# Branch A's scores: products over 64 rows, one component on each half of TensorE's rows, in place of products over 128 rows

## The chip, the cores and the metric

The kernel runs on one core of one Trainium2 chip. The metric is the device time of one execution in microseconds (us): the median of the timed runs. All times in the text are from these runs, or from one execution that the hardware profiler recorded.

## The reference, cut to what is computed

One layer of a streaming encoder with two attention branches beside each other, for a prompt of 2048 frames and for 8 running streams of 16 new frames with 512 cached frames each. The change concerns branch A alone, and of it the prompt's frames:

```python
D_MODEL, SEQ, CHUNK, Q_BLOCK = 1024, 2048, 64, 128
N_HEADS_A, HEAD_DIM_A = 4, 64

def diff_attention(q, k, v, qpos, kpos, lam):          # q, k: (b, s, heads, 2 components, 64)
    s = einsum('bqhcd,bkhcd->bhcqk', q, k) * (HEAD_DIM_A ** -0.5)
    mask = (kpos // CHUNK)[None, :] <= (qpos // CHUNK)[:, None]
    p = softmax(where(mask, s, -inf), axis=-1)
    w = p[:, :, 0] - lam * p[:, :, 1]
    return einsum('bhqk,bkhe->bqhe', w, v)             # v: (b, s, heads, 128)
```

Each of the four heads has two components c (0 and 1) with 64 numbers each for a query and for a key. The scores are a product over these 64 numbers for each component. Branch B (stick-breaking attention, eight heads of 64) has scores of the same shape with other weights behind them. Before the attention stand a norm and a projection (2048 x 1024 by 1024 x 6144), behind it gates, two branch products and one output product.

## The kernel before, in words

**Number format.** A float32 operand is cut into two fp16 halves, `hi` and `lo` (`split`: ScalarE writes hi = scale * x, VectorE writes lo = scale * x - hi). A product of two such numbers is made of three: hi*hi, hi*lo and lo*hi.

**Units and tiles.** The attention is done in eight units u of two heads of B or one head of A: even units are branch A (`kind` 0), odd ones branch B (`kind` 1). A unit has 17 steps, one for each tile t of 128 rows: the sample tile (t = NT = 16) first, and then the 16 prompt tiles. Per step there are
- `project`: 24 matmuls of 512 columns into a bank "mm" of PSUM, most steps 24 more for the gates into bank "t"; then in `finish` the rotation of q and k on GpSimd (A only), and the cutting into halves: `query` for q, `halves` for k and v;
- `transpose_qk`: TensorE turns the halves of q and k into bank "t", 128 x 128 a block, and ScalarE (A) or VectorE (B) copies them into `kst` (k) and `qst` (q), which have the 64 numbers along the rows;
- `scores`: for prompt tile t there are t // 4 + 1 chunks of 512 keys (the last one of 128 to 512). Its inner `chunk(c, ch)` makes one component's (in B: one head's) scores of one chunk in one bank "s". In the last chunk, the mask is added by one more product;
- `evacuate` (A): VectorE reads the bank, scales it into the score buffer and keeps the largest value; behind the last chunk `softmax_pair` queues exp, sums, the difference of the two components, its halves and their turn by a DMA, and 27 cost units later the products with v (`pv_block`), three a block of 128 keys.

**A's operands before.** k is turned as two blocks, one for each component, with rows [hi 64; lo 64]. q is turned as four blocks: for each component [hi; hi] and [lo; 0]. So the first product of `chunk` (L708) gives hi*hi + hi*lo over 128 rows and the second (L709) lo*hi, with 64 rows times zero:

```python
            T.matmul(p[:, 0:n], qst[:, c, :], kk[:, c, 0:n], start=True, stop=False)
            T.matmul(p[:, 0:n], qst[:, 2 + c, :], kk[:, c, 0:n], start=False, stop=not diag)
```

**What sets the order.** Pieces of the projection, the scores and the products with v are interleaved by costs that the code gives them (`interleaved`, `give`, `later_on`). The framework then puts each engine's instructions in order by its own model of the time; an engine runs them in that order. `kept` holds an instruction in the order of the code. PSUM has 8 banks: 2 "mm", 3 "s", 1 "t", 2 "o". A buffer taken anew waits until its last reader is done, so the fourth score bank taken waits for the evacuation of the first.

## Time and profile before

| | |
|---|---|
| timed runs | 2225.53 us median of 3 (2224.59 to 2226.76) |
| the profiled execution: its time, first to last instruction | span 2223.5 us (no other time of it is recorded) |
| TensorE matmuls, busy | 2061.2 us (93%), 14608 matmuls |
| TensorE weight loads, busy (beside the matmuls) | 1110.4 us (50%) |
| VectorE, busy | 1743.8 us (78%) |
| ScalarE, busy | 1606.2 us (72%) |
| GpSimd, busy | 699.6 us (31%) |
| mean granted TensorE clock | 0.980 |

The span lies about 2 us below the median of the timed runs. A matmul's record has a length in which its way through the array is included (383 ns for 512 columns), and the records of a stream overlap: the next starts 216 ns after the one before. So what a matmul costs in a stream is read from starts in the timeline, not from its length. PE is TensorE's matmuls, PEld its weight loads, DVE VectorE, ACT ScalarE, POOL GpSimd.

### The profile page before, as it was taken

The page shows a single profiled execution, that of the slowest core. Times are in us where ns is not written, and L with a number is a line of the kernel's source. Part 1 is how long each engine was busy: PE and PEld are TensorE (multiplying, and loading weights), DVE is VectorE, ACT ScalarE, POOL GpSimd, SP SyncE. Part 2 cuts the span into 40 slices and gives each one's busy share as a digit, 9 for nine tenths or more (in the row PEclk, how much of TensorE's full clock was granted, in tenths as well). Part 3 has the DMA queues.
Part 4 walks back from the last instruction along what each step waited for, and adds up shares of the span by engine and source line. Part 5 has one row for each costly group of instructions (what it writes and reads, how often), then busy time and mean ns, then how long its engine had stood idle before and what let it go on. Part 6 is the DMA issues. An engine that isn't in the chain of part 4 may idle for free. (4 is left out here: it accounts for less than half of the span.)

```text
span 2223.5 us, 41495 instructions
## 1 busy us (share of the span) xinstructions
PE 2061.2 (93%) x14608; PEld 1110.4 (50%) x14608; DVE 1743.8 (78%) x3799; ACT 1606.2 (72%) x3212; POOL 699.6 (31%) x608
## 2 busy tenths in 40 slices
PE   5999999999999999999999998989998788899997
PEld 3655555555555455555554554555454444444443
DVE  4667869789887788988778888777789877787864
ACT  3978677789877677978677788876688666666531
POOL 1232014356410443742024355301334412111210
PEclk8999999999999999999999999999999899999999
DMA  9778559899796889979879999985787999999762
GB/s 323 258 241 201 120 139 217 181 227 203 200 252 158 222 201 202 207 205 221 198 195 216 191 224 207 241 181 130 159 170 155 201 280 255 230 254 224 194 166 67
DMA packets 824978, 451.05 MB, mean 203 GB/s; under 512 B 556122, under 2 KB 763274, under 8 KB 824256
## 3 DMA queue, kind: packets, MB, share of 16 engines
q1 hardware_dynamic: 823820, 448.01, 82.7%
q8 instruction: 114, 1.87, 0.3%
q14 instruction: 96, 0.79, 0.1%
q10 hardware_dynamic: 948, 0.39, 0.1%
HBM read 229.87 MB, written 86.02 MB: 142 GB/s over the span
## 5 line engine op out<-in xcount | busy, mean ns | idle before, releaser
L688 POOL TENSOR_TENSOR sc_p<-sc_p,sc_n 128x127 f32<-128x127 f32 (+7 forms) x192 | 313.3, 1635 | 663.1 <-DVE sc_n L682 510.6
L467 PEld LDWEIGHTS <-hs 128*128 128x128 f16 x3120 | 293.3, 99 | 318.5 <-issue 6.4
L467 PE MATMUL ps_mm<-wa,hs 128*128 128x512 f16 x1590 | 391.2, 382 | 5.3 <-DMA hs<-hT_d 5.0
L467 PE MATMUL ps_mm<-wb,hs 128*128 128x512 f16 x1530 | 377.4, 380 | 0.0
L682 DVE TENSOR_TENSOR_SCAN sc_n<-ps_s,sc_n,zero_t 128x512 f32<-128x512 f32 x192 | 245.4, 1278 | 33.3 <-ACT ps_s L134 28.1
L708 PE MATMUL ps_s<-k,qst 128*128 128x512 f16 (+3 forms) x640 | 223.2, 350 | 30.0 <-DVE sc_n L682 22.8
L543 PEld LDWEIGHTS <-hs 128*128 128x128 f16 x1632 | 155.0, 98 | 181.7 <-DVE qst L576 5.1
L543 PE MATMUL ps_t<-wa,hs 128*128 128x512 f16 x1020 | 242.3, 380 | 2.1 <-DVE qst L576 2.0
L619 DVE TENSOR_TENSOR sc_n<-sc_p,sc_n 128x128 f16<-128x128 f32 (+7 forms) x192 | 217.7, 1137 | 32.9 <-ACT sc_n L616 32.3
L134 ACT ACTIVATE sc_p<-ps_s,usc 128x512 f32<-128x512 f32 (+3 forms) x320 | 203.9, 637 | 34.4 <-PE ps_s L709 23.0
L709 PE MATMUL ps_s<-k,qst 128*128 128x512 f16 (+3 forms) x640 | 223.6, 350 | 0.0
L616 ACT CAST sc_n<-sc_p 128x128 f16<-128x128 f32 (+7 forms) x192 | 155.0, 809 | 57.3 <-POOL sc_p L688 55.8
L134 ACT ACTIVATE ps_s<-ps_s,usc 128x512 f32<-128x512 f32 (+3 forms) x320 | 196.3, 613 | 0.0
L543 PE MATMUL ps_t<-wb,hs 128*128 128x512 f16 x612 | 151.7, 383 | 4.8 <-DMA hs<-hT_d 2.1
L769 PE MATMUL ps_o<-v,wt 128*128 128x128 f16 x1088 | 135.2, 224 | 22.1 <-DMA wt<-sc_n 21.9
L1535 PE MATMUL ps_o<-wo,wb 128*128 128x512 f16 x624 | 141.6, 382 | 1.1 <-ACT wb L1309 1.1
L602 DVE TENSOR_SCALAR_CACHE_REDUCE sc_p<-ps_s,usc 128x512 f32<-128x512 f32 (+3 forms) x160 | 106.2, 664 | 35.7 <-PE ps_s L709 20.5
L770 PE MATMUL ps_o<-v,wt 128*128 128x64 f16 x1088 | 127.1, 196 | 0.0
L769 PEld LDWEIGHTS <-wt 128*128 128x128 f16 x1088 | 101.0, 100 | 50.1 <-DMA wt<-sc_n 25.3
L682 DVE TENSOR_TENSOR_SCAN sc_n<-ps_s,zero_t 128x128 f32<-128x128 f32 (+3 forms) x128 | 104.0, 813 | 27.7 <-ACT ps_s L134 27.7
L1501 PEld LDWEIGHTS <-wa 128*128 128x128 f16 x816 | 77.7, 98 | 94.2 <-issue 4.1
L1544 POOL TENSOR_TENSOR x<-m,x 128x512 f32<-128x512 f32 x32 | 45.6, 1427 | 247.1 <-DVE m L1539 138.7
(378 smaller groups left out, 4548.6 us busy)
## 6 DMA issues: line engine op xcount, KB each, us to landing
hs<-hT_d SPq DMA_DIRECT2D x132, 512.0 KB
g_d<-gt SPq DMA_DIRECT2D x68, 256.0 KB
out_dram<-pr SPq DMA_DIRECT2D x204, 64.0 KB
o_d<-o SPq DMA_DIRECT2D x136, 64.0 KB
wa<-g_d SPq DMA_DIRECT2D x17, 512.0 KB
wb<-g_d SPq DMA_DIRECT2D x17, 512.0 KB
hs<-o_d SPq DMA_DIRECT2D x17, 512.0 KB
wide<-in_w_ada_dram SPq DMA_DIRECT2D x8, 1024.0 KB
```

The source lines that it names most:

```text
L134: i = S.activation(**kw)
L467: T.matmul(box["p"], box["h"][:, hi, k, :], U["w"][k][:, wi, :], start=(n == 0), stop=(n == 3 * KT - 1))
L543: x = T.matmul(box["g"][:, 0:gw], box["h"][:, hi, k, :], U["wg"][k // per][:, k % per, wi, :], start=(j == 0), stop=(j == 3 * KT - 1))
L616: x = S.copy(out=hi, in_=src)
L619: V.tensor_tensor(out=lo, in0=src, in1=hi, op=ALU.subtract)
L682: V.tensor_tensor_scan(out=dst[:, lo : lo + n][:, ::-1], data0=src[:, 0:n][:, ::-1], data1=zero_t[:, 0:1].to_broadcast([P, n]), initial=fi ...
L688: G.tensor_tensor(out=p[:, 0:m], in0=p[:, 0:m], in1=n[:, 1 : m + 1], op=ALU.mult)
L708: T.matmul(p[:, 0:n], qst[:, c, :], kk[:, c, 0:n], start=True, stop=False)
L709: T.matmul(p[:, 0:n], qst[:, 2 + c, :], kk[:, c, 0:n], start=False, stop=not diag)
L769: T.matmul(po[:, c * P : (c + 1) * P], wt[:, wj, :], vt[:, c, :, :], start=first, stop=False)
L770: T.matmul(po[:, c * P : c * P + 64], wt[:, nb + wj, :], vt[:, c, 0, :], start=False, stop=last)
L1535: T.matmul(po, st["y"][:, yi * 8 + k, :], wo[j * 4 + k // 2][:, wi, k % 2, :], start=(n == 0), stop=(n == 3 * KT - 1))
```

## The change

For the prompt tiles of branch A only:
- q and k are cut into halves so that one block has the hi halves of both components and one the lo halves (`by_half`: columns c = 0, then c = 1, taken in the same buffers). `query`'s doubled hi (128 x 256 on ScalarE) becomes a plain cut of 128 x 128.
- `transpose_qk` turns four blocks (k hi, k lo, q hi, q lo), not six, and the copy of q has 256 columns, not 512. Behind the turn, rows 0 to 63 are component 0 and rows 64 to 127 component 1.
- `pair(ch)` replaces `chunk(0, ch)` and `chunk(1, ch)`: it takes two banks "s" at once, then issues a product of one column into the first bank (128 rows; its result is overwritten), six products of 64 rows (three a component, the components in turn, in the order of the code by `kept`), the masks in the last chunk, and both evacuations.

B's scores and the sample tile's are as before.

```diff
+    def by_half(qb, k16):
+        return qb[:, 0, :, :, :].rearrange("p c r d -> p c (r d)"), k16.rearrange("p c f d -> p c (f d)")
...
-                query(rot[:, 0:128], s)
-                halves(k16, rot[:, 128:256], s)
+                if t == NT:
+                    query(rot[:, 0:128], s)
+                    halves(k16, rot[:, 128:256], s)
+                else:
+                    qn, kn = by_half(qb, k16)
+                    split(qn[:, 0, :], qn[:, 1, :], rot[:, 0:128], s, S)
+                    split(kn[:, 0, :], kn[:, 1, :], rot[:, 128:256], s, S)
...
+        paired = U["kind"] == 0 and t < NT
+        if paired:
+            qn, kn = by_half(q16, k16)
+            for j, x in enumerate((kn[:, 0, :], kn[:, 1, :], qn[:, 0, :], qn[:, 1, :])):
+                T.transpose(pt[:, j * P : (j + 1) * P], x, id16)
...
-        copy(out=qst, in_=pt[:, 256:768].rearrange("p (j n) -> p j n", j=4))
+        nq = 2 if paired else 4
+        copy(out=qst, in_=pt[:, 256 : 256 + nq * P].rearrange("p (j n) -> p j n", j=nq))
...
+        def pair(ch):
+            job = own[0]
+            seg = job["segs"][ch * 4 // SEG]
+            n = 512 if ch < t // 4 else (t % 4 + 1) * P
+            ps = [bank("s"), bank("s")]
+            qst, kk = U["q", t], U["k"][ch]
+            diag = ch == t // 4
+            T.matmul(ps[0][:, 0:1], idb, mask_a[:, 0:1], start=True, stop=True)
+            for i, (qf, kf) in enumerate(((0, 0), (0, 1), (1, 0))):
+                for c in (1, 0):
+                    rows = slice(c * 64, c * 64 + 64)
+                    x = T.matmul(ps[c][:, 0:n], qst[rows, qf, :], kk[rows, kf, 0:n], start=(i == 0), stop=(i == 2 and not diag))
+                    kept(x)
+            if diag:
+                for c in range(2):
+                    T.matmul(ps[c][:, n - 64 : n], idb, mask_a, start=False, stop=True)
+            for c in range(2):
+                evacuate(job, seg, c, ps[c], ch * 512 - seg["lo"] * P, n, sc[:, 3:4], sc[:, 4:5], ch)
+            if diag:
+                softmax_pair(job)
...
+        if kind == 0:
+            return [(4.0 if ch < t // 4 else t % 4 + 1.0, lambda ch=ch: pair(ch)) for ch in range(nch)]
```

In the built program the order of all engines is laid out anew. Three places show it. (In the rows, the line of the code comes first, then the operation, out<-in and the size; the number behind a name counts buffers as they are taken, so two numbers of ps_s are two banks taken.)

TensorE, unit 0, tile 5, the first chunk of 512 keys, component 0. Before, its two products (L708, L709) stand between products with v (L765 to L767), and those of component 1 come 48 rows later:

```order
L767 LDWEIGHTS wt_1585
L767 MATMUL ps_o_1982<-v_912,wt_1585 128x128
L708 LDWEIGHTS qst_1686
L708 MATMUL ps_s_1734<-k_977,qst_1686 128x512
L709 LDWEIGHTS qst_1686
L709 MATMUL ps_s_1734<-k_977,qst_1686 128x512
L765 LDWEIGHTS wt_1591
L765 MATMUL ps_o_1991<-v_912,wt_1591 128x128
```

The same chunk now, from the second round of its six products (L764) on; ahead of these rows stand a projection's matmul and the first round:

```order
L764 LDWEIGHTS qst_1693
L764 MATMUL ps_s_1768<-k_975,qst_1693 128x512
L764 LDWEIGHTS qst_1693
L764 MATMUL ps_s_1767<-k_975,qst_1693 128x512
L764 LDWEIGHTS qst_1693
L764 MATMUL ps_s_1768<-k_975,qst_1693 128x512
L764 LDWEIGHTS qst_1693
L764 MATMUL ps_s_1767<-k_975,qst_1693 128x512
L760 LDWEIGHTS idb_194
L760 MATMUL ps_s_1800<-masks_196,idb_194 128x1
L471 LDWEIGHTS hs2_182
L471 MATMUL ps_mm_2522<-wa3_172,hs2_182 128x512
```

The six stand together (in 157 of the 160 pairs; in three, one matmul of one column of L235 stands between the second and the third round). The product of one column (L760) behind them is that of the next pair: it writes bank 1800, which is taken after 1767 and 1768.

TensorE, unit 0, tile 9, the last chunk (256 keys), and tile 10 behind it. Before, other work stands between component 0 and component 1 of tile 9, and again between tile 9 and tile 10 (7 products with v behind the rows shown):

```order
L712 MATMUL ps_s_2275<-masks_196,idb_194 128x64
L765 LDWEIGHTS wt_2100
L765 MATMUL ps_o_2500<-v_912,wt_2100 128x128
L766 LDWEIGHTS wt_2100
L766 MATMUL ps_o_2500<-v_912,wt_2100 128x128
L767 LDWEIGHTS wt_2100
L767 MATMUL ps_o_2500<-v_912,wt_2100 128x128
L708 LDWEIGHTS qst_2140
L708 MATMUL ps_s_2308<-k_2021,qst_2140 128x256
L709 LDWEIGHTS qst_2140
L709 MATMUL ps_s_2308<-k_2021,qst_2140 128x256
```

Now:

```order
L764 MATMUL ps_s_2330<-k_2041,qst_2162 128x256
L768 LDWEIGHTS idb_194
L768 MATMUL ps_s_2330<-masks_196,idb_194 128x64
L768 LDWEIGHTS idb_194
L768 MATMUL ps_s_2331<-masks_196,idb_194 128x64
L760 LDWEIGHTS idb_194
L760 MATMUL ps_s_2379<-masks_196,idb_194 128x1
L764 LDWEIGHTS qst_2299
L764 MATMUL ps_s_2380<-k_975,qst_2299 128x512
L764 LDWEIGHTS qst_2299
L764 MATMUL ps_s_2379<-k_975,qst_2299 128x512
```

Tile 10's pair follows directly, and its bank 2380 is the one that 2330 was in (three banks in turn). Of the 156 distances from a pair's end to the next pair of the same unit, 8 have less than 1 us of TensorE's work in them (5 of them in unit 0); before, 26 of 156 distances from one chunk's component 0 to the next chunk's had less than 1.2 us.

VectorE, unit 0, tiles 1 and 2. Before, the evacuations (L602) of the two components of tile 1 (256 keys) have nine other rows between them:

```order
L602 TENSOR_SCALAR sc_p_1457,mx_1459<-ps_s_1453,usc0_702 128x256
L636 TENSOR_REDUCE nm_1447<-mx_1440 128x2
L323 SCALAR_TENSOR_TENSOR wb0_1426<-wa7_176,sw_1515,wb0_1426 128x512 x2
L323 SCALAR_TENSOR_TENSOR wb1_1427<-wa6_175,sw_1515,wb1_1427 128x512 x2
L323 SCALAR_TENSOR_TENSOR wb2_1428<-wa5_174,sw_1515,wb2_1428 128x512 x2
L323 SCALAR_TENSOR_TENSOR wb3_1429<-wa4_173,sw_1515,wb3_1429 128x512
L502 SCALAR_TENSOR_TENSOR qbuf1_214<-rot_1846,sq0_711,qbuf1_214 128x2x64
L323 SCALAR_TENSOR_TENSOR wb3_1429<-wa4_173,sw_1515,wb3_1429 128x512
L323 SCALAR_TENSOR_TENSOR k16_1844<-rot_1846,sq0_711,k16_1844 128x2x64
L650 RECIPROCAL r_1450<-l_1449 128x2
L602 TENSOR_SCALAR sc_n_1458,mx_1459<-ps_s_1472,usc0_702 128x256
```

Now (L620 is the same instruction) they follow each other:

```order
L323 SCALAR_TENSOR_TENSOR sc_n_1438<-sc_p_1437,r_1445,sc_n_1438 128x128
L620 TENSOR_SCALAR sc_p_1461,mx_1463<-ps_s_1450,usc0_702 128x256
L620 TENSOR_SCALAR sc_n_1462,mx_1463<-ps_s_1451,usc0_702 128x256
L243 TENSOR_SCALAR sc_q_1498<-ps_t_1496 128x1
L371 COPY fsq_1507<-ps_t_1496 128x1
```

The cutting of the next unit's weights (L323 on wb) has gone to another place.

More of the change, by code (lines that the diff above doesn't have):

```diff
@@ L572, in transpose_qk @@
             U["q", t] = qst = stg.tile([P, 4, P], F16, tag="qst", name="qst", bufs=Q_BUFS)
+            if paired:
+                qst = qst[:, 0:2, :]
             kst = U["k"][g][:, :, i * P : (i + 1) * P]
```

16 lines of the change are left out of this document (8 added, 8 removed).

## The prediction

> **What bounds the kernel now.** I read the page first (busy time by engine), then the busy time in the four stretches in which branch A's scores run, TensorE's waits, the groups by line and shape, and the timeline for what a matmul costs in a stream.
>
> ```profile
> span 2223.5 us, 41495 instructions
> PE 2061.2 (93%) x14608; PEld 1110.4 (50%) x14608; DVE 1743.8 (78%) x3799; ACT 1606.2 (72%) x3212; POOL 699.6 (31%) x608
> core 0: us, PE busy (x) PEld busy (x) DVE busy (x) ACT busy (x) POOL busy (x), PEclk, DMA share, GB/s
> sum 685.00, PE 648.40 PEld 360.22 DVE 558.26 ACT 516.63 POOL 169.37; mean PE 162.10 PEld 90.06 DVE 139.57 ACT 129.16 POOL 42.34
> ```
>
> The last row sums the stretches 130 to 295, 530 to 700, 940 to 1112 and 1354 to 1532 us, the units of branch A. TensorE is busy 648.4 of 685.0 us there, VectorE 81%, ScalarE 75%. So in the stretches that the change touches TensorE is the bound, all other engines together make it idle for 36.6 us, and a microsecond of TensorE's stream is worth nearly a microsecond of time. What it waits for:
>
> ```profile
> PE ps_o L769 <- DMA wt<-sc_n: 21.9, 11, 4.2
> PE ps_o L765 <- DMA wt<-sc_n: 18.3, 14, 5.6
> PE ps_s L708 <- DVE sc_n L602: 4.9, 4, 1.5
> PE ps_s L708 <- DVE sc_p L602: 0.5, 1, 0.5
> ```
>
> (us in total, times, longest.) L765 is branch A's product with v, late for the turn by DMA; L602 is the evacuation of A's scores, for which the next score bank waits: 5.4 us in all, five times.
>
> **The change part by part.** Branch A has four units of 16 tiles with t // 4 + 1 chunks, 40 chunks a unit, 160 in all: 112 of 512 keys and 16 each of 384, 256 and 128. The groups by shape agree (A and B have half each):
>
> ```profile
> L708 PE MATMUL ps_s<-k,qst 128*128 128x512 f16 x448 | 171.5, 383 | 22.8 <-DVE sc_n L682 15.7 <-DVE sc_n L602 4.9 <-DVE csc L951 1.4
> L708 PE MATMUL ps_s<-k,qst 128*128 128x384 f16 x64 | 20.9, 326 | 4.4 <-DVE sc_n L682 4.4
> ...
> 1004.21 0.38 PE L708 MATMUL ps_s<-k,qst 128*128 128x512 f16 x1
> 1004.43 0.38 PE L709 MATMUL ps_s<-k,qst 128*128 128x512 f16 x1
> 1004.65 0.19 PE L712 MATMUL ps_s<-masks,idb 128*128 128x64 bf16 x1
> 1004.67 1.24 PE L467 MATMUL ps_mm<-wb,hs 128*128 128x512 f16 x5
> ...
> 1006.62 0.28 PE L561 MATMUL ps_t<-id,k 128*128 128x128 f16 x2
> 1006.73 0.39 PE L565 MATMUL ps_t<-id,qbuf 128*128 128x128 f16 x4
> 1006.95 0.22 PE L765 MATMUL ps_o<-v,wt 128*128 128x128 f16 x1
> ```
>
> From the starts in the timeline: 512 columns cost (1004.65 - 1004.21) / 2 = 0.22 us, and by the five in a row behind them (1.24 - 0.38) / 4 = 0.215; I use 0.216; the six turns 0.33 / 6 = 0.056 each; the mask of 64 columns 0.03. By proportion 384 columns cost 0.162, 256 cost 0.108, 128 cost 0.056.
>
> *Products.* Before, a chunk is four products: 0.864 us at 512 keys, 0.648, 0.432, 0.224 at the smaller ones. Now it is six of 64 rows. No product on half of the rows next to one on the other half stands in this trace. The nearest rows are products on quarters of TensorE's columns (L860, L883), which are issued in the same way, four in turn, and those with few rows (L1489):
>
> ```profile
> L860 PE MATMUL ps_s<-dks,qpad 128*32 128x512 f16 x256 | 16.8, 381 | 2.9 <-ACT wa L1309 2.9
> ...
> 1807.76 1.24 PE L1535 MATMUL ps_o<-wo,wb 128*128 128x512 f16 x5
> 1808.93 1.05 PE L860 MATMUL ps_s<-dks,qpad 128*32 128x512 f16 x16
> ...
> 1828.31 1.06 PE L1308 MATMUL ps_s<-id,hs 128*128 128x128 f16 x16
> 1829.30 0.84 PE L883 MATMUL ps_t<-v16c,dwt 128*32 128x256 f16 x24
> 1830.07 1.25 PE L1535 MATMUL ps_o<-wo,wb 128*128 128x512 f16 x5
> ...
> 1770.84 1.24 PE L1501 MATMUL ps_mm<-wb,wa 128*128 128x512 f16 x5
> 1772.01 1.12 PE L1489 MATMUL ps_t<-gsm,ones 1*128 1x512 f32 x2
> ```
>
> Sixteen products of 512 columns on quarters take 1.05 us with the last one's length of 0.38: four rounds, (1.05 - 0.38) / 3 = 0.22 a round. So four parts of the array run at once, and a round costs what one matmul does, 0.218. I take the same for two halves of the rows: three rounds a pair, 0.654 at 512 keys. The other end is that they don't overlap: six times 0.216.
>
> *Switches.* The same rows show what it costs to change how the array is divided. Five products of L1535 from 1807.76 are done by 1807.76 + 5 x 0.216 = 1808.84, and L860 starts at 1808.93: 0.09 us. Sixteen turns from 1828.31 end at 1829.21, L883 starts at 1829.30: 0.09; six rounds of 0.109 end at 1829.96, the next full matmul starts at 1830.07: 0.10. For rows instead of columns, L1501's five end at 1771.92 and L1489, on one row, starts at 1772.01: 0.09 again. So a pair pays 0.19 us, in and out. Nothing hides it: TensorE streams on both sides.
>
> [...]
>
> *One-column product (L760).* One a pair; nearest row the mask of 64 columns, 0.03 us. Its wait for a bank stands ahead of everything behind it on TensorE: see the banks below.
>
> *Sum of a pair:* 0.654 + 0.19 + 0.03 = 0.874 against 0.864 at 512 keys, + 0.01, times 112 is + 1.1 us. At 384: 0.164 x 3 + 0.22 = 0.712, + 0.064; at 256: 0.55, + 0.118; at 128: 0.39, + 0.166; together 0.348 x 16 = + 5.6. Three pairs are split by a matmul of full rows (L235) and switch twice more: + 0.6. In all + 7.3 us. The gain of a quarter of the products (29 us) is eaten by 160 x 0.22 = 35 us of switches and one-column products.
>
> *Turns.* Two fewer a tile: 64 x 2 x 0.056 = 7.2 us less on TensorE, all of it in its stream. Products and turns together: + 0.1 us.
>
> *ScalarE.*
>
> ```profile
> L576 ACT COPY qst<-ps_t 128x512 f16<-128x512 f16 x64 | 38.8, 606 | 0.0
> L575 ACT COPY k<-ps_t 128x256 f16<-128x256 f16 x64 | 24.0, 375 | 2.1 <-PE ps_t L565 2.1
> L501 ACT ACTIVATE qbuf<-rot,sq 128x256 f16<-128x256 f32 x68 | 34.7, 510 | 3.2 <-POOL rot L513 2.7
> L318 ACT ACTIVATE k<-rot,sq 128x128 f16<-128x128 f32 x68 | 27.3, 402 | 10.4 <-PE ps_t L561 10.4
> ```
>
> The copy of q goes from 606 ns to that of k's width, 375; the hi half from 510 to 402: 64 x 0.339 = 22 us less on an engine busy 75% there. No wait of TensorE for ScalarE stands among the rows above, so I count 1 us. VectorE's lo halves have as many elements as before; DMAs, SP and POOL have the same work.
>
> *Banks.* Of three score banks a pair takes two at once, so its second waits for the first evacuation of the pair before; a chunk before waited for the one three back.
>
> ```profile
> L602 DVE TENSOR_SCALAR_CACHE_REDUCE sc_p<-ps_s,usc 128x512 f32<-128x512 f32 x112 | 83.4, 745 | 30.0 <-PE ps_s L709 20.5 <-PE ps_s L712 9.0
> L602 DVE DVE_READ_ACCUMULATOR sc_p<-ps_s,usc 128x1 f32 x160 | 12.9, 81 | 0.0
> ```
>
> An evacuation takes 0.745 + 0.081 = 0.83 us and starts when the last product is through (0.16 us behind its stream, 0.38 - 0.22). So behind a pair the next must stand 1 us off or TensorE stops, with all that is queued behind it (projection, turns, products with v). In the order of the changed kernel 8 of 156 distances are shorter: at the 1.2 us that a wait took before (4.9 / 4) that is 9 us if none is softened, and half of it, 5 us, is near the 5.4 us that go away. I take + 1 us, between - 5 (all bank waits gone, since pairs stand further apart elsewhere) and the rival below.
>
> *Sum:* 2223.5 + 0.1 - 1 + 1 = 2223.6, and with 2 us between span and median as before, 2226 us by the timed runs: no change. (About 0.2%, 4.5 us, is what a measurement of this kernel can tell from none.)
>
> **Rivals.**
> 1. *Waits go (faster).* ScalarE is relieved by 22 us of 517 and pairs stand further apart (8 close ones, 26 before). If a third of the 36.6 us of idle TensorE goes, 12 us are saved: 2214 us. For it: the rows of L708 and ScalarE's load. Against it: half of the idle time (18.3 us) is L765's, which waits for the turn by a DMA, and the change leaves that.
> 2. *The second bank (slower).* VectorE is busy 81%; where a long instruction stands ahead of the first evacuation, the pair waits that much longer. If 16 of the 156 pairs wait the 1.2 us of a wait before, that is 19 us against 5.4: + 14, 2240 us. It decides from 9 waits on ((4.5 + 5.4) / 1.2 = 8.3). For it: 8 pairs are too close already. Against it: the other distances are mostly over 2 us, two evacuations.
> 3. *Weights aren't hidden between products of one half (slower).* A round of L860 would show it and doesn't (0.22 with four loads), but these load 32 columns each, a pair's 128. Exposed twice a pair at the 0.1 us of a switch, that is 160 x 0.2 = 32 us: 2258 us. [...]
> 4. *The change doesn't do what it says: halves of rows don't run at once.* Six times 0.216 + 0.22 is 1.516 for 0.864 at 512 keys: 112 x 0.652 = 73 us; at 384, 256 and 128 it is 0.544, 0.436 and 0.332 more, times 16, 21 us. With the split pairs' 0.6 and less the turns' 7.2 that is + 87: 2313 us. For it: no row here has two halves of rows at work. Against it: four quarters of columns do run at once.
> [...]
>
> **How the numbers follow.** Forecast (TensorE's sum is nil, waits within 4 us) 0.36; rival 1, 0.29; rival 5, 0.04; rival 2, 0.22; rival 3, 0.06; rival 4, 0.03. Faster by over 0.2% is 0.29 + 0.04 = 0.33, within it 0.36, slower 0.22 + 0.06 + 0.03 = 0.31. The likeliest is 2226; its own range is 2221 to 2230. The range of 8 in 10 takes in rivals 1 and 2 with their spread of some 8 us about 2214 and 2240: 2206 to 2248; outside are rivals 3 to 5 (0.13) and the tails of 1 and 2.
>
> **What would show it.** Right: products of L764 in three rounds of 0.22 us, two starts a few ns apart; 0.09 us ahead of a pair and 0.10 behind it; a full pair 0.87 us from the matmul ahead to the one behind; turns four a tile; TensorE's busy time in A's stretches unchanged to a few us; its waits for L620 (the evacuation) below 10 us. Wrong: rounds of 0.3 us or more (rivals 3, 4); a gap ahead of pairs other than 0.09; waits of L760 and L764 for VectorE of 15 us and more (rival 2); idle time in A's stretches that falls by 10 us (rival 1). The forecast also falls if the new order of all engines moves the waits in branch B's units, which no row of the profile before can tell.

## The result, and the profile after

The changed kernel takes 2306.89 us (median of 4 runs, 2303.14 to 2309.48), the kernel before 2225.06 us beside it: a ratio of 1.0372, with a 95% interval of 1.0357 to 1.0388. It is slower, by 82 us; the forecast was 2226, the range ended at 2248. One execution of 4331 us, of the run E18 below, is left out of its median. The profiled execution, from its page (span, busy time by engine, and the chain that ended last):

```profile
span 2301.3 us, 42229 instructions
PE 2101.7 (91%) x14960; PEld 1082.7 (47%) x14960; DVE 1764.6 (77%) x3799; ACT 1585.5 (69%) x3212; POOL 715.3 (31%) x608
PE 41%; DVE 19%; DMA 15%; ACT 13%; issue 7%; POOL 3%; SPq 1%; DVEq 0%; POOLq 0%; ACTq 0%
```

TensorE's share of the span fell, and the busy times of the other engines are within 21 us of those before. TensorE's own busy time rose by 40 us (2061.2 before) and its idle time by 37 (162 before, 200 now), though its sum in the prediction is nil. The time at half clock rose from 90 to 153 us (see the table below); that would make some 31 of the 40 us (an estimate: half of the 63 us more, since products of 128 columns started 0.107 us apart at half clock and 0.057 at the full one, by the timeline at the end). The chain passes through four engines and the DMAs, none with half of it. Lines have moved: A's evacuation L602 is now L620, B's scores L708 are L726, B's scan L682 is L700, the products with v L765 and L769 are L806 and L810, the projection L467 is L471, the gates L543 are L552.

**A pair by itself is what was forecast.** TensorE's timeline around one pair of 512 keys (start, length to the end of the last, group):

```profile
1067.11 2.97 PE L471 MATMUL ps_mm<-wb,hs 128*128 128x512 f16 x13
1070.01 0.82 PE L764 MATMUL ps_s<-k,qst 64*128 64x512 f16 x6
1070.77 0.18 PE L760 MATMUL ps_s<-masks,idb 128*128 128x1 bf16 x1
1070.80 0.27 PE L573 MATMUL ps_t<-id,k 128*128 128x128 f16 x2
1070.91 0.27 PE L573 MATMUL ps_t<-id,qbuf 128*128 128x128 f16 x2
```

Thirteen projection products end at 1067.11 + 13 x 0.216 = 1069.92, the pair starts 0.09 us later. From its start to the next full matmul are 0.76 us: six products in three rounds (0.65) and 0.10 to switch back. So 0.85 us with both switches, 0.88 with the one-column product (forecast 0.874). Four blocks are turned where there were six. ScalarE's two steps shrank as forecast (groups by shape; 606 and 510 ns before):

```profile
L594 ACT COPY qst<-ps_t 128x256 f16<-128x256 f16 x64 | 25.2, 393 | 0.0
L318 ACT ACTIVATE qbuf<-rot,sq 128x128 f16<-128x128 f32 x64 | 26.1, 409 | 4.7 <-POOL rot L517 4.7
```

**The waits grew, but not at the pair.** TensorE's longest (total, times, longest):

```profile
PE ps_s L726 <- DVE sc_n L700: 48.3, 44, 3.0
PE ps_o L810 <- DMA wt<-sc_n: 26.8, 18, 4.2
PE ps_o L806 <- DMA wt<-sc_n: 22.9, 18, 2.7
...
PE ps_s L764 <- DVE sc_n L620: 5.5, 8, 1.3
```

L764, the pair, waits 5.5 us for its banks in this row, and 7.6 with two shorter rows (1.4 us of L764 and 0.7 of L760); that was forecast at below 10. Branch B's scores wait 48 us for the scan that reads their banks; the row was 22.8 us before:

```profile
PE ps_s L708 <- DVE sc_n L682: 22.8, 25, 2.2
```

**Where the time is.** I cut both executions at the first score tile of each unit: four stretches of A, three of B (B's fourth runs into the end). Busy time of all engines, the sums; A's four and then B's three, before:

```profile
sum 700.00, PE 663.40 PEld 365.54 DVE 557.46 ACT 533.85 POOL 168.70; mean PE 165.85 PEld 91.38 DVE 139.36 ACT 133.46 POOL 42.17
...
sum 702.00, PE 668.25 PEld 361.88 DVE 591.44 ACT 567.78 POOL 328.35; mean PE 222.75 PEld 120.63 DVE 197.15 ACT 189.26 POOL 109.45
```

and after:

```profile
sum 781.00, PE 742.34 PEld 367.05 DVE 558.37 ACT 517.27 POOL 155.82; mean PE 185.59 PEld 91.76 DVE 139.59 ACT 129.32 POOL 38.95
...
sum 711.00, PE 634.77 PEld 338.10 DVE 614.37 ACT 567.06 POOL 350.96; mean PE 211.59 PEld 112.70 DVE 204.79 ACT 189.02 POOL 116.99
```

A's stretches are 81 us longer, B's three 9 us; the rest is 12 shorter, which makes the 78 us between the spans. And A's stretches hold work that was in B's. The projection's products alone in A's four stretches (length, matmuls' busy time and count, loads', clock), before (1495 products):

```profile
136.00:301.00 165.00, 80.76 (x348) 33.02 (x349) 0.99 0.69 174
531.00:705.00 174.00, 90.70 (x384) 36.17 (x385) 1.00 0.85 208
940.00:1118.00 178.00, 91.42 (x382) 36.25 (x382) 0.99 0.85 206
1355.00:1538.00 183.00, 89.30 (x381) 36.03 (x382) 0.98 0.83 195
```

and after (1708):

```profile
135.00:324.00 189.00, 93.72 (x392) 37.31 (x390) 0.97 0.62 159
558.00:755.00 197.00, 101.28 (x438) 41.04 (x438) 0.99 0.75 193
991.00:1191.00 200.00, 102.44 (x438) 41.24 (x438) 0.99 0.77 190
1432.00:1627.00 195.00, 103.17 (x440) 41.15 (x440) 0.99 0.76 186
```

That is 213 products or 46 us (x 0.216) more. The gates' products were 120 in each stretch before; now they are 144 in three of them and 120 in the fourth, 72 or 16 us more:

```profile
558.00:755.00 197.00, 32.56 (x144) 13.57 (x144) 0.99 0.75 193
...
1432.00:1627.00 195.00, 27.97 (x120) 10.99 (x120) 0.99 0.76 186
```

In the order this shows as a delay: A's last tile was scored at projection step 22.0, 56.0, 90.0 and 124.1 of the kernel's 136, and now at 25.0, 58.8, 92.8 and 126.9 (24 products a step). B's stretches have 33 us less of TensorE's busy time and are no shorter. The mean granted clock fell from 0.980 to 0.967.

### The profile page after: what moved, and what is told of

Read it like the earlier page. It is cut to its first block, busy times and chain, and to the rows that moved or that the text cites. A ratio compares the mean times of both kernels' runs of the same rounds, so it can differ in the third digit from the quotient of the medians.

```text
span 2301.3 us, 42229 instructions
## 1 busy us (share of the span) xinstructions
PE 2101.7 (91%) x14960; PEld 1082.7 (47%) x14960; DVE 1764.6 (77%) x3799; ACT 1585.5 (69%) x3212; POOL 715.3 (31%) x608
## 4 chain that ended last, share of the span: by engine, by line
PE 41%; DVE 19%; DMA 15%; ACT 13%; issue 7%; POOL 3%; SPq 1%; DVEq 0%; POOLq 0%; ACTq 0%
PE ps_mm L471 13%; PE ps_t L552 8%; DMA wt<-sc_n 6%; PE ps_o L1576 5%; DVE sc_n L700 4%; PE ps_mm L1542 4%; ACT sc_p L134 3%; PE ps_s L764 2%; ACT junk L298 2%; POOL sc_p L706 2%; ACT sc_n L134 1%; DVE sc_n L323 1%; DVE sc_p L675 1%; DVE sc_n L637 1%; DVE sc_n L620 1%
## 5 line engine op out<-in xcount | busy, mean ns | idle before, releaser
L706 POOL TENSOR_TENSOR sc_p<-sc_p,sc_n 128x127 f32<-128x127 f32 (+7 forms) x192 | 323.5, 1687 | 480.6 <-DVE sc_n L700 471.7
L471 PEld LDWEIGHTS <-hs 128*128 128x128 f16 x3120 | 294.7, 99 | 333.3 <-issue 29.2
L471 PE MATMUL ps_mm<-wa,hs 128*128 128x512 f16 x1590 | 393.8, 386 | 3.4 <-DMA hs<-hT_d 3.0
L471 PE MATMUL ps_mm<-wb,hs 128*128 128x512 f16 x1530 | 377.3, 385 | 3.6 <-DMA hs<-hT_d 2.2
L700 DVE TENSOR_TENSOR_SCAN sc_n<-ps_s,sc_n,zero_t 128x512 f32<-128x512 f32 x192 | 245.4, 1278 | 38.5 <-ACT ps_s L134 32.2
L637 DVE TENSOR_TENSOR sc_n<-sc_p,sc_n 128x128 f16<-128x128 f32 (+7 forms) x192 | 239.7, 1252 | 23.9 <-ACT sc_n L634 23.7
L552 PEld LDWEIGHTS <-hs 128*128 128x128 f16 x1632 | 156.4, 100 | 194.0 <-issue 14.1
L552 PE MATMUL ps_t<-wa,hs 128*128 128x512 f16 x1020 | 242.8, 385 | 3.3 <-DVE qst L594 2.1
L726 PE MATMUL ps_s<-k,qst 128*128 128x512 f16 (+3 forms) x320 | 112.4, 352 | 59.1 <-DVE sc_n L700 48.3
L810 PE MATMUL ps_o<-v,wt 128*128 128x128 f16 x1088 | 137.3, 225 | 26.9 <-DMA wt<-sc_n 26.8
L552 PE MATMUL ps_t<-wb,hs 128*128 128x512 f16 x612 | 154.3, 390 | 7.9 <-DVE qst L594 3.1
L620 DVE TENSOR_SCALAR_CACHE_REDUCE sc_n<-ps_s,usc 128x512 f32<-128x512 f32 (+3 forms) x160 | 106.6, 666 | 49.6 <-PE ps_s L764 49.5
L134 ACT ACTIVATE sc_p<-sc_p,nm 128x1024 f32<-128x1024 f32 (+4 forms) x96 | 85.8, 894 | 75.8 <-DVE nm L654 75.8
L620 DVE TENSOR_SCALAR_CACHE_REDUCE sc_p<-ps_s,usc 128x512 f32<-128x512 f32 (+3 forms) x160 | 106.5, 666 | 30.1 <-PE ps_s L768 29.7
L810 PEld LDWEIGHTS <-wt 128*128 128x128 f16 x1088 | 102.3, 101 | 57.6 <-DMA wt<-sc_n 33.7
L512 POOL TENSOR_TENSOR rot<-pr,rope 128x256 f32<-128x256 f32 x68 | 62.0, 912 | 207.9 <-ACT pr L485 126.7
```

The costliest lines, as they stand in the source:

```text
L134: i = S.activation(**kw)
L471: T.matmul(box["p"], box["h"][:, hi, k, :], U["w"][k][:, wi, :], start=(n == 0), stop=(n == 3 * KT - 1))
L552: x = T.matmul(box["g"][:, 0:gw], box["h"][:, hi, k, :], U["wg"][k // per][:, k % per, wi, :], start=(j == 0), stop=(j == 3 * KT - 1))
L620: V.tensor_scalar(out=dst[:, lo : lo + n], in0=p[:, 0:n], scalar1=sc_pos, scalar2=None, op0=ALU.mult, op1=ALU.max, accum_out=job["mx"][:, ...
L637: V.tensor_tensor(out=lo, in0=src, in1=hi, op=ALU.subtract)
L700: V.tensor_tensor_scan(out=dst[:, lo : lo + n][:, ::-1], data0=src[:, 0:n][:, ::-1], data1=zero_t[:, 0:1].to_broadcast([P, n]), initial=fi ...
```

## The experiments

Each run's text says what its theory numbers mean. The table gives medians, the ratio to the kernel before on the same chip with its interval, the length of A's four and B's three stretches, and the time at half clock, summed from the trace's clock records. The lengths are from the exact starts; the windows shown are cut at whole microseconds and differ by up to 2. A pin is a call of `kept`, which holds an instruction in the order of the code. The lead of E8 and E18 is the number of projection steps that are written ahead of a score tile, 5 before. A change whose interval doesn't contain 1 is clear of noise, also where it is under 2%.

| run | us | ratio | A's four | B's three | half clock |
|---|---|---|---|---|---|
| before | 2225 | | 700 | 703 | 90 |
| after | 2306.9 | 1.0372 (1.0357-1.0388) | 780 | 712 | 153 |
| E1 pair of full rows | 2322.9 | 1.0440 (1.0411-1.0470) | 799 | 709 | 157 |
| E2 after, 4 score banks, 1 output | 2321.7 | 1.0442 (1.0421-1.0463) | 751 | 705 | 162 |
| E3 E1 with E2's banks | 2320.7 | 1.0453 (1.0424-1.0483) | 731 | 731 | 184 |
| E4 E2, one half after the other | 2328.1 | 1.0477 (1.0459-1.0495) | 753 | 709 | 162 |
| E5 after, projection pinned | 2357.0 | 1.0602 (1.0575-1.0628) | 806 | 716 | 205 |
| E6 E1, projection pinned | 2337.9 | 1.0508 (1.0477-1.0539) | 772 | 730 | 199 |
| E7 E1 without pins | 2254.0 | 1.0127 (1.0094-1.0160) | 697 | 720 | 112 |
| E8 before, lead 6 in A | 2250.2 | 1.0118 (1.0086-1.0149) | 727 | 704 | 111 |
| E9 after, 4 score, 1 projection bank | 2420.0 | 1.0913 (1.0868-1.0957) | 789 | 743 | 249 |
| E10 before with E9's banks | 2432.4 | 1.0951 (1.0920-1.0981) | 774 | 750 | 241 |
| E11 before, A's products pinned | 2238.3 | 1.0077 (1.0048-1.0105) | 699 | 716 | 105 |
| E12 after without pins | 2295.7 | 1.0335 (1.0298-1.0371) | 763 | 710 | 103 |
| E13 after, 4 banks shared | 2307.5 | 1.0383 (1.0364-1.0401) | 772 | 703 | 182 |
| E14 before with E13's banks | 2302.6 | 1.0362 (1.0339-1.0385) | 768 | 710 | 175 |
| E15 E1 with E13's banks | 2319.6 | 1.0431 (1.0409-1.0452) | 774 | 708 | 180 |
| E16 before, A one product less | 2235.3 | 1.0061 (1.0038-1.0084) | 684 | 712 | 158 |
| E17 before, B one product less | 2243.0 | 1.0101 (1.0083-1.0119) | 698 | 714 | 154 |
| E18 before, lead 3 in A | 2279.5 | 1.0264 (1.0241-1.0287) | 689 | 734 | 137 |

### E1 to E4: is it the halves?

E1 keeps the pair with its pins and takes the old operands, six turns a tile and four full products:

```diff
-                if t == NT:
+                if True:
...
-        paired = U["kind"] == 0 and t < NT
+        paired = False
...
-            for i, (qf, kf) in enumerate(((0, 0), (0, 1), (1, 0))):
+            for i in range(2):
                 for c in (1, 0):
...
-                    x = T.matmul(ps[c][:, 0:n], qst[rows, qf, :], kk[rows, kf, 0:n], ...)
+                    x = T.matmul(ps[c][:, 0:n], qst[:, 2 * i + c, :], kk[:, c, 0:n], ...)
                     kept(x)
```

> The changed kernel's pair (two score banks taken at once, the products of a pair pinned together, the one-column product ahead of them), but with the operands of before: two products of 128 rows a component, six blocks turned a tile. No product of 64 rows is left. Theory 1 (taking two of three banks at once makes the scheduler put branch A's scores two to three projection steps later; branch B's scores then lack work to fill TensorE's waits): its order is as late as the changed kernel's, so it takes about as long, 2290 to 2315 us. Theory 2 (the products on half of the rows, or the switches around them, cost the 80 us, directly or by the granted clock): near the kernel before, 2220 to 2235 us.

E2 is the changed kernel, E3 is E1, both with `"s": 4, "o": 1` in BANKS.

> The changed kernel with four score banks and one output bank in place of three and two, all else as it is. In its order branch A's last scores stand at the same projection step as before the change. Theory 1: the loss goes, 2215 to 2245 us (one output bank may cost up to 20 us). Theory 2: the products of 64 rows and their switches are all there, so it stays at 2290 to 2315 us.

> E1's full-row pair with the four score banks and the one output bank of E2: the control for E2, which differs from it only in the products, turns and copies. By the prediction's sum (a pair on halves costs 0.01 us more at 512 keys, the turns give it back) E2 and E3 lie within 8 us of each other; theory 1 puts both near 2225 us. Theory 2: E3 is 60 to 90 us faster than E2.

E4 is E2 with the two loops exchanged, so that a component's three products stand behind each other and then the other's.

> E2 with the six products of a pair ordered by component (three on one half of the rows, then three on the other), so that only the third and the fourth can run at once. If two halves of rows run at once as the rounds in the changed kernel's trace show, each pair has two rounds more: 2 x (112 x 0.216 + 16 x 0.326) = 59 us more than E2 if TensorE's time counts in full (40 to 65). If the halves gained nothing by running at once, it equals E2 within 8 us.

E1 has no product of 64 rows and no switch, and is slower than the changed kernel. So the loss needs neither halves nor switches. It doesn't need the long waits of B's scores for the scan either: that row, 48.3 us in the changed kernel, is 28.4 us in E1. E2 against E3, 2321.7 and 2320.7, says what halves are worth against full rows in the same pair with the same banks: nothing, as the sum of the prediction said. But the two orders aren't the same (A's stretches 751 and 731 us, B's 705 and 731), and neither run came near the 2225 us that theory 1 gave them. E2 brings A's last tile back to steps 22.0, 56.0, 90.0, 124.0 and B's three stretches to 705 us, but the missing output bank costs elsewhere, and without a control it doesn't tell how much. E4 should have cost 59 us if the halves ran in program order; it costs 6. That isn't because halves gain nothing side by side, as its expectation reads such a result: its pair still takes 0.76 us to the next full matmul:

```profile
1023.20 0.83 PE L764 MATMUL ps_s<-k,qst 64*128 64x512 f16 x6
1023.96 0.28 PE L573 MATMUL ps_t<-id,k 128*128 128x128 f16 x2
```

### E5 to E8: is it the order?

E5 (on the changed kernel) and E6 (on E1) pin the projection so that it can't run ahead of the pairs; A's last tile is then at the same projection steps as in the kernel before:

```diff
-            T.matmul(box["p"], box["h"][:, hi, k, :], U["w"][k][:, wi, :], ...)
+            x = T.matmul(box["p"], box["h"][:, hi, k, :], U["w"][k][:, wi, :], ...)
+            if n % 6 == 0 and kind == 1:
+                kept(x)
```

> The changed kernel, with one edit: every sixth product of branch B's projection is pinned behind the TensorE instruction that the program issues before it, so the projection can't run ahead of A's scores. Pairs stay as they are (163 groups of 64-row products, 480 rounds). In the order, A's last tile is scored at projection step 22.0, 56.0, 90.0, 124.0 of its unit, as before the change (25.0, 58.8, 92.8, 126.9 with it). Theory 1 (the change's loss is the order: A's scores come some three steps later, branch B's units then have too little projection left to fill TensorE's waits, and its clock falls in the gaps): units 1, 3 and 5, which lost 28 to 31 us each, lose under 8 each, the time at half clock falls from 152 us to about 100, and the whole takes 2210 to 2240 us. Theory 2 (the pair itself: two banks, two evacuations side by side, whatever the order): 2290 to 2310 us, the same units lose. Theory 3 (the pins hold TensorE up, since it then waits for a pair with no projection to run in between): over 2310 us, with the loss in units 0, 2, 4, 6.

> The same pins on the pair with full rows (old operands, six turned blocks a tile, four full products a pair and no switch of TensorE's rows). A's last tile at step 21.5, 55.5, 90.0, 124.0. Theory 1: 2215 to 2245 us, within 20 of the half-row kernel with the same pins; against the full-row pair without them (2323) it gains 80 or more. Theory 2: 2310 or more, as without the pins. Theory 3: over 2320 us.

E7 is E1 without `kept(x)` in the pair: its products may go as soon as their own bank is free.

> The full-row pair without its own pins and without pins elsewhere: the four products of a pair may be issued when their own bank is free, so a pair falls into two chunks in the order, though both evacuations are still written one behind the other and the one-column product stays. A's last tile at step 22.2, 56.2, 90.2, 124.2, as before the change. Theory 1: 2220 to 2240 us (160 one-column products cost about 6). Theory 2 (what the pair asks of VectorE): about 2320, as with the pins.

E8 changes one number of the kernel before:

```diff
-        target = position(len(steps) * past / whole + LEAD)
+        lead = LEAD + (1.0 if n < len(steps) and steps[n][0] % 2 == 0 and steps[n][0] > 0 else 0.0)
+        target = position(len(steps) * past / whole + lead)
```

> The kernel before with only its lead (how much projection is written ahead of a score tile) raised from 5 to 6 in A's units from the second on. No product changes. A's last tile is scored one step of projection later in units 2, 4, 6 (57.0, 91.0, 125.0), unit 0 as before (22.0). Theory 1, in proportion to the steps (28 to 31 us for three steps): units 3 and 5 lose some 10 us each, the kernel 2235 to 2250 us; if the loss begins only where the projection runs out, less. Theory 2: no loss, 2220 to 2228 us.

Theory 1 in its simple form fell with E5 and E6: the place in the order is as before and the loss is larger. Theory 3's numbers came out (over 2310 and over 2320 us). A's stretches now hold no more projection than before, and TensorE stands still in them instead. A's four stretches of E5, all engines (columns: length, then TensorE, its loads, VectorE, ScalarE, GpSimd, and the granted clock), and then, from its waits, those at the pair:

```profile
137.00:331.00 194.00, 168.01 (x1166) 82.70 (x1166) 127.59 (x361) 111.38 (x264) 25.49 (x32) 0.91 0.59 146
566.00:771.00 205.00, 179.25 (x1304) 91.33 (x1303) 141.14 (x395) 131.88 (x305) 45.82 (x48) 0.93 0.70 176
sum 805.00, PE 702.63 PEld 352.94 DVE 546.24 ACT 507.79 POOL 151.43; mean PE 175.66 PEld 88.23 DVE 136.56 ACT 126.95 POOL 37.86
```

```profile
PE ps_s L766 <- DVE sc_n L622: 31.2, 25, 5.2
PE ps_s L766 <- DVE sc_p L622: 11.2, 11, 2.1
```

102 us idle and a clock of 0.91 to 0.95, with 42 us of waits at the pair for A's evacuation where the changed kernel has 7 (5.5 and 1.4). So the pair does lack banks when nothing else stands between pairs. That the changed kernel's order covers this with B's projection fits the two tables, but the pins of E5 may cost something of their own.

E7 is the clearest single run: E1's products, the one-column product and both evacuations, but no pins, and some 70 of E1's 100 us are gone. A's stretches are at 697 us again:

```profile
sum 697.00, PE 656.59 PEld 364.99 DVE 551.74 ACT 518.80 POOL 161.22; mean PE 164.15 PEld 91.25 DVE 137.94 ACT 129.70 POOL 40.30
```

Its time is still 14 us above the range that theory 1 gave it. E8 is the kernel before with A one step later: + 25 us, all in A's stretches (700 to 727), as expected of the total but not of the place.

### E9 to E12: the second bank

E9 and E10: `"mm": 1, "s": 4` in BANKS, on the changed kernel and on the one before.

> The changed kernel with a fourth score bank, taken from the projection (one bank for it where there were two; both output banks stay). Beside its control, the kernel before with the same banks (next run); the two stand at nearly the same place in the order (A's last tile at step 21, 55, 89, 123 and 22, 55, 89, 123). Theory 1b (the runs so far have turned theory 1 into this: a pair that is issued as one takes two of three banks at once, so TensorE needs other work between pairs; the order gives it branch B's projection, or, where that is pinned, it waits): with four banks a pair no longer waits for the pair ahead of it, so this kernel is within 20 us of its control, where the difference with three banks was 81. Theory 2b (the pair's cost lies elsewhere: its switches, its two evacuations in a row, the clock): it is 60 us or more over its control.

> The control: the kernel before with four score banks and one projection bank. Both theories: 2240 to 2320 us, since a projection tile must be emptied before the next starts; what counts is the difference to the run above.

E11, on the kernel before, with its own products:

```diff
-            T.matmul(p[:, 0:n], qst[:, c, :], kk[:, c, 0:n], start=True, stop=False)
+            x = T.matmul(p[:, 0:n], qst[:, c, :], kk[:, c, 0:n], start=True, stop=False)
+            if kind == 0:
+                kept(x)
```

(and the same for the second).

> The kernel before, with its own products, each of branch A's two products a chunk pinned behind the TensorE instruction written before it, so that the pins are there but no product waits for a second bank. A's last tile at step 23.0, 56.9, 90.9, 125.0, one later than before. Theory 1b: 2235 to 2255 us, as with the lead of 6 (2250). If the pins themselves were the cause: 2290 us or more.

E12 is the changed kernel without the line `kept(x)`.

> The changed kernel without its pins: a component's three products may be issued as soon as their own bank is free. In the order the 64-row products fall into 271 groups (163 with pins), 220 of them of one component alone, 830 rounds (480) and 654 switches (438); A's last tile at 22.3, 56.3, 90.3, 124.3, as before the change. By the prices of a round (0.218 us at 512 keys) and a switch (0.095) TensorE has some 60 us more of rounds and 20 of switches than with the pins. Theory 1b: the waits in branch B's units go (its loss falls from 117 us to about 60), and the time is 2290 to 2330 us, made of rounds and switches. Theory 2b: the waits stay and it takes 2370 us or more.

With four score banks the changed kernel is 12 us faster than its control, where it was 82 slower with three. But the control is far slower than I expected of it (2432 against at most 2320), so something else sets the time there. E11: pins on products that need one bank cost 19 us. E12 has 350 more rounds and 216 more switches than the changed kernel, some 80 us of TensorE's time by their prices, and is no slower (11 us less, with intervals that overlap). Against the kernel before its time is 76 us longer, in the range that theory 1b gave it, and TensorE's busy time 85 us (2061.2 and 2146.1); so here the work added on TensorE shows nearly in full, and dropping the pins doesn't help the pair on halves as it helped E1. In its B stretches TensorE is as busy as before the change (672 and 668 us, clock 0.99), and yet the three last 711 us, 9 more than before and as long as in the changed kernel. One of the three, and the sum:

```profile
738.00:976.00 238.00, 223.13 (x1580) 120.50 (x1578) 196.96 (x319) 188.78 (x392) 112.30 (x88) 0.99 0.89 204
...
sum 711.00, PE 671.85 PEld 362.09 DVE 594.51 ACT 569.62 POOL 337.94; mean PE 223.95 PEld 120.70 DVE 198.17 ACT 189.87 POOL 112.65
```

### E13 to E15: four banks, no bank taken away

The bank of the turns joins those of the scores:

```diff
-    BANKS = {"mm": 2, "s": 3, "t": 1, "o": 2}
+    BANKS = {"mm": 2, "s": 4, "o": 2}
...
+        buf = "s" if tag == "t" else tag
-        return ps.tile([P, 512 if dt == F32 else 1024], dt, tag=tag, ..., bufs=BANKS[tag])
+        return ps.tile([P, 512 if dt == F32 else 1024], dt, tag=buf, ..., bufs=BANKS[buf])
```

> The changed kernel with one pool of four banks for scores and turns (before: three for scores, one for turns); projection and output keep two each. No pair is split in the order (160 groups, 480 rounds, 416 switches), and A's last tile is scored at step 22.0, 56.0, 90.0, 124.0, as in the kernel before. Theory 1b (the loss is the second bank's): within 20 us of its control E14, 2205 to 2250 us; by the prediction's sum 7 us of turns and some 5 us of shorter full pairs against dearer small ones, it could be a few us faster. Theory 2b (the pair costs elsewhere): 60 us or more over E14.

> The control: the kernel before with the same pool of four banks for scores and turns. Both theories: 2205 to 2260 us; a turn may now wait for a score's evacuation, a score has a fourth bank when no turn runs.

> The pair with full rows and its pins (E1) with the same pool. Theory 1b: within 20 us of E14 too, 75 or more below E1 (2323). Theory 2b: 2300 us or more. The difference to E13 is the change's own products and turns, without the banks: by the prediction's sum nil, -10 to +10 us.

Again the pair costs nothing beside its control: 2307.5 and 2302.6. But the control itself lost 78 us, 43 more than the end of the range that I gave it, though its order has A's last tile within 0.6 of a step of where it was. So a bank arrangement can take the same 80 us as the change without any pair, and the two controlled comparisons show that the costs don't add, not that a pair is free. E13 against E15: halves are 12 us better than full rows here. E15 was to lie 75 us below E1 if the loss is the second bank's; it lies 3 below (2319.6 and 2322.9).

### E16 to E18: does TensorE bound anything?

E16 leaves out the second product of each of A's chunks (the low half of q), E17 that of B's: 320 products, 59 us of TensorE's stream each (half of 640 products, of 0.216 us at 512 keys and less at the smaller ones).

```diff
+            if kind != 0:
                 T.matmul(p[:, 0:n], qst[:, 2 + c, :], kk[:, c, 0:n], start=False, stop=not diag)
```

> The kernel before without the second product (the low half of q) of each of branch A's score chunks: 320 products, 59 us of TensorE's stream, all in A's four stretches; the scores lose their low half. Theory 3 (TensorE bounds A's stretches, not B's): A's four stretches fall from 700 to 640 to 665 us, the whole to 2165 to 2190. Theory 4 (TensorE bounds both, and B's stretches lasted for the waits and the low clock alone): the same for this run. If VectorE's evacuations bound A instead: 2205 or more.

> The same for branch B: the second product of its chunks left out, again 320 products and 59 us of TensorE's stream, 44 of them in its first three stretches. Theory 3: B's three stretches stay within 15 us of 702, and the whole takes 2200 to 2225 us. Theory 4: they fall by 35 to 44 us, the whole to 2165 to 2185 us.

E18 is E8 with -2.0 in place of + 1.0.

> The kernel before with its lead lowered from 5 to 3 in A's units from the second on: A's last tile at step 55.8, 89.8, 124.0 (56.0, 90.0, 124.1 before), B's first at 56.0, 90.0, 124.0 (56.5, 90.5, 124.5): at most half a step of projection, 2.6 us, a unit goes from A's stretch to B's. Theory 3: 2215 to 2228 us, no change or a few us faster. Theory 4: no change.

Both theories fell. The kernel with 59 us less work for TensorE is 15 us slower, or 22. Part of the 59 us went to the clock: TensorE's busy time fell by 30 us (2061.2 to 2031.5 in E16), and the time at half clock rose from 90 to 158. Leaving products out also lays out the order anew, and what that costs by itself wasn't measured. E16's stretches, A and then B (clock 0.95 in A):

```profile
1355.00:1530.00 175.00, 154.85 (x1099) 85.32 (x1096) 138.23 (x385) 135.42 (x308) 42.26 (x46) 0.95 0.83 201
sum 683.00, PE 612.04 PEld 338.27 DVE 547.18 ACT 508.28 POOL 165.46; mean PE 153.01 PEld 84.57 DVE 136.79 ACT 127.07 POOL 41.36
...
sum 713.00, PE 677.14 PEld 364.91 DVE 594.55 ACT 581.13 POOL 328.93; mean PE 225.71 PEld 121.64 DVE 198.18 ACT 193.71 POOL 109.64
```

TensorE is busy 51 us less in A's stretches and they are 17 us shorter; B's three are 11 us longer, and what follows A's fourth another 23. The third branch of E16's expectation, that VectorE's evacuations bound A, fits its time; but over the whole run TensorE's waits for them rose from 5.4 to 18 us, and those for a turn by DMA ahead of the products with v from 40 to 54, so the trace doesn't single them out. E17's three B stretches, with 44 us of products fewer, are 714 us, but other work moved in:

```profile
sum 715.00, PE 659.36 PEld 355.55 DVE 601.35 ACT 569.54 POOL 332.71; mean PE 219.79 PEld 118.52 DVE 200.45 ACT 189.85 POOL 110.90
```

TensorE is busy 659 us there for 668 before, so E17 doesn't tell by itself whether TensorE bounds B. E18 moves at most half a step from A to B and costs 59 us, more than E8's whole step the other way, where 2215 to 2228 us were expected. None of the 18 runs is faster than the kernel before, so there is no version that beats both.

## Why the prediction was wrong

**The first step failed: "a microsecond of TensorE's stream is worth nearly a microsecond of time".** It was read from 648 of 685 us busy. E16 takes 59 us of stream out of just these stretches; they get 17 us shorter, and the kernel becomes 15 us slower. The stretches are filled by whatever the order puts into them; that the filled engine is also the one that ends them was never in the row. Work put in does count (E12: 85 us busier, 76 us slower), so TensorE isn't free either. The sum of TensorE's prices was right in each term that could be measured, but it was no sum of time, because it took the order of everything else for granted.

**The step that made the error: the term for the banks.** I took the changed order as given, counted 8 pairs too close in it and priced their waits at + 1 us. The waits at the pair came out at 7.6 us, as written. But that order had already paid for the second bank: 285 products of projection and gates, 62 us, stand in A's stretches more than before, and B's stretches don't shrink for it. With a fourth score bank (E2) or, on full rows, without the pins (E7) A's last tile stands where it stood before. "Busy time in A's stretches unchanged to a few us" was what should have shown it; it rose by 79. I compared the distances of pairs in the new order and not the place of A's tiles against the projection, which shows a delay of three steps. The price of moved work was nil in my sum, and a sentence at the end left it open.

**Rival 2 had the right resource, and the wrong size and place.** The second bank matters: E5 shows 42 us of waits for it once the order doesn't cover them, and E1 against E7 shows 69 us that hang on issuing the full-row pair as one. I gave it + 14 us, from 16 waits of 1.2 us.

**What held.** The price of a pair (0.88 us for 0.874 forecast), of a switch, of the turns and of ScalarE's steps. That products and turns together are worth nothing held within some 20 us, with either sign: halves against full rows in a pinned pair are 16 us faster (changed kernel and E1), 1 slower (E2, E3), 19 slower (E5, E6) and 12 faster (E13, E15). Without pins halves are 42 us slower (E12, E7), with 830 rounds in place of 480. Rival 1 fell: TensorE stands still for 39 us in A's stretches (781.00 - 742.34), as it did before (37). Rival 5, that switches are free in a pair, fell with its two gaps, 0.09 and 0.10 us. Rival 4 fell in the timeline: halves do run at once (six products in 0.82 us, 0.38 of it the last one's length), and its 2313 us lies near the measured time by chance. Rival 3 fell too: the 960 loads of 64 rows took 94 ns each, and two of them exposed in a pair would be 0.19 us; 0.76 us for three rounds of 0.216 and a switch of 0.10 leaves no room for them:

```profile
L764 PEld LDWEIGHTS <-qst 64*128 64x128 f16 x960 | 34.6, 94 | 68.6 <-issue 48.5 <-ACT qbuf L318 0.4
```

**What is shown, and what stays open.** Shown: the loss needs no 64-row product (E1); on full rows it goes for the most part when the pair's products needn't be issued as one (E7); with a fourth score bank the pair costs nothing on top of its control (E9 and E10, E13 and E14), though each control is slow itself; and the kernel before loses 19 to 78 us by small changes of order or banks alone (E8, E11, E14, E18), and 213 with one projection bank (E10). Argued only: that the 62 us of work moved into A's stretches are the loss; the sizes agree, but E16 forbids to read them as one for one. Not told apart: which part of the 69 us is the second bank's and which the pins'; pins alone cost 19 us on products of one bank (E11). Open: which chain sets the time in a moved order. It isn't the low clock alone: E17 has as much of it as the changed kernel (154 us) and is 64 us faster, E12 has 103 us and is only 11 faster. It isn't TensorE's stream alone, for less of it gives no time back (E16, E17). No run has the order of before under the new pair without a pin elsewhere or other banks.

## What to carry to other kernels

An engine that is 95% busy is not thereby the bound: where a scheduler fills waits with work that has time, busy shares look the same whether the engine ends the stretch or only fills it; take work out once, as E16 does (59 us of stream less, 15 us slower), and put some in, as E12 does (85 us busier, 76 us slower), before a sum of its microseconds is called time. Where a change makes instructions claim two buffers at once, look in the new order for what stands between them and where it was before: the price shows as work that moved, not as waits at the claim. And in a kernel whose order is computed, a change whose parts cost nothing has still the order as its largest term; here small moves cost 0.8 to 3.6% (E8, E11, E14, E18), with either sign of the move.

## What the runs showed of the hardware that I had not expected

**Halves ran out of program order.** In E4 the program has three products of one half, then three of the other. In the trace the starts of a pair of 512 keys come in twos: in 46 of the 112 such pairs they are exactly at 0, 10, 226, 236, 442 and 452 ns from the first. In 88 of the 112 the two products that release the banks, the third and the sixth of the program, are the last two (in 16 more, the mask's product releases them). So each half worked through its own products there, and in those 46 pairs the fourth of the program started 10 ns behind the first. That an engine runs its instructions in the order laid out, which the expectation of E4 took for granted, didn't hold for these products.

**The clock halved after a wait of 2.54 us.** The wait stands in the timeline of the changed kernel, with products behind it at either clock:

```profile
654.94 0.23 PE L806 MATMUL ps_o<-v,wt 128*128 128x128 f16 x1 [2.54 <-DMA wt<-sc_n]
...
655.51 0.22 PE L807 MATMUL ps_o<-v,wt 128*128 128x128 f16 x1
655.57 0.22 PE L808 MATMUL ps_o<-v,wt 128*128 128x128 f16 x1
655.62 0.22 PE L806 MATMUL ps_o<-v,wt 128*128 128x128 f16 x1
655.68 0.22 PE L807 MATMUL ps_o<-v,wt 128*128 128x128 f16 x1
...
656.30 0.31 PE L808 MATMUL ps_o<-v,wt 128*128 128x128 f16 x1
656.41 0.31 PE L806 MATMUL ps_o<-v,wt 128*128 128x128 f16 x1
656.51 0.31 PE L807 MATMUL ps_o<-v,wt 128*128 128x128 f16 x1
656.62 0.31 PE L808 MATMUL ps_o<-v,wt 128*128 128x128 f16 x1
```

and the busy times around it (length, TensorE, its loads, VectorE, ScalarE, GpSimd, clock):

```profile
645.00:656.20 11.20, 8.66 (x71) 4.62 (x69) 9.29 (x29) 9.92 (x27) 1.12 (x1) 0.98 0.83 217
656.20:659.60 3.40, 3.23 (x23) 1.65 (x23) 1.02 (x3) 3.23 (x11) 0.00 (x0) 0.56 0.86 233
659.60:670.00 10.40, 10.40 (x59) 4.60 (x56) 9.44 (x26) 5.55 (x11) 2.20 (x1) 1.00 0.46 135
```

After 2.54 us of waiting the granted clock is near half for 3.4 us (0.56 in the stretch shown); by the clock record from 655.80 to 659.21, so it begins 0.86 us after the wait ended. The starts of the products go from 0.057 us apart ((655.68 - 655.51) / 3) to 0.107 ((656.62 - 656.30) / 3). The clock records of the changed kernel have 26 stretches at half clock, all but one of them 3.41 us or a multiple long, against 16 before. Ahead of 25 of the 26, TensorE had stood still for 1.9 us or more of the last 6.8 (twice 3.41), in one wait or in several; whether every such wait halves the clock was not counted.
